# RWKV-7's triangular inverse: from GpSimd steps by way of DRAM to 32x32 products on TensorE, with other durations in the kernel's ordering estimate

## The chip, the core and the metric

The kernel runs on one core of one Trainium2 chip. The metric is the device time of one execution in microseconds. The kernel before takes 3022.41 us (median of 3 runs, 3020.9 to 3025.26). A core has five engines with queues of their own: TensorE (PE, products into PSUM), VectorE (DVE), ScalarE (ACT), GpSimd (POOL), and SyncE (SP), whose queue issues most transfers. In the profile PEld is TensorE's loading of the stationary operand.

## The reference

One inference step of two layers over 512 tokens of a prompt and 32 tokens of a sample, 1024 features, all float32. Layer 0 is half SwiGLU, RG-LRU beside retention, memory attention, half SwiGLU. Layer 1 is half SwiGLU, RWKV-7 time mixing, memory attention, half SwiGLU. The part that the change touches is the time mixing's recurrence over 16 heads of 64 features:

```
def step(S, inp):
    r_t, w_t, k_t, v_t, kk_t, b_t = inp
    sa = jnp.einsum('bhvk,bhk->bhv', S, -kk_t)
    S = S * w_t[:, :, None, :] + sa[..., None] * b_t[:, :, None, :] + v_t[..., None] * k_t[:, :, None, :]
    return S, jnp.einsum('bhvk,bhk->bhv', S, r_t)
```

The kernel computes it by chunks of 32 tokens. Within a chunk, the corrections U of all tokens solve (I + N) U = right-hand side for each head, where N is a strictly triangular 32x32 matrix of products between tokens. So each head and chunk needs the inverse of I + N once.

## The kernel before

**Halves and streams.** The 544 tokens are two halves: A (256) and B (256 of the prompt and the 32 of the sample). Features lie on partitions, tokens in columns. Every linear layer runs over granules of weights, 128 output columns each: a transfer of 512 KB into a raw buffer (`wr`), a rounding to float32r on ScalarE, a subtraction for the low part on VectorE or GpSimd (`W<-wr,W`), then 24 products. Around layer 1's mixing A is 42 granules ahead of B, so that one half's products fill the other half's waits. There are five weight slots and three raw buffers; `wkv` borrows three slots and one raw buffer for its own tiles (`K.lend(3, 1)`) until it is through.

**The order of the work.** The program is a set of generators (tasks). A planner (`Clock.op`, `Kern.plan`, `Kern.run`) estimates when each instruction could start and gives it that time as its priority, so the estimate sets each engine's order, which of VectorE and GpSimd takes an `ett` operation, and which weights are loaded when. Its durations are formulas in `mm`, `_v`, `gtt`, `act` and others. Engines then serve their queues in that order.

**The RWKV stage.** `wkv` starts five tasks over nine blocks: four of A's with 64 tokens, four of B's with 64 tokens, and the sample's 32 tokens. A block is two chunks (the last one).

- `wkv_prep` makes decays, keys and values of a block on VectorE and ScalarE and, for each chunk, 16 products `KL x X` whose masked result lands in the lower half of `X`. Rows 96 to 127 hold N. It sends N of each chunk to DRAM (`dn`).
- `wkv_solve` loads N from DRAM so that a partition holds one head, one chunk and a quarter of the rows (`P<-dn`), sets Z to the identity, and does 31 steps of elimination, each a GpSimd product and a GpSimd subtraction. Z goes back through DRAM (`dz`) into the diagonal blocks of 128x128 tiles (`w.tb`, two of them, zeroed once), by four transfers, half of them on ScalarE's queue. It waits until the chain of two blocks before is through.
- `wkv_load` transposes keys and values for the chain.
- `wkv_chain` runs the chunks in order: right-hand side (`pr`, 16 products), ScalarE's copy to `RS`, the inverse's use (`pu`, four 128x128 products), four reads, the new state (`b1`, 16 products and four VectorE operations), the output (16 products).
- `wkv_norm` does the heads' norm and gate, mostly on GpSimd.

B's blocks come in the same tasks behind A's, and need B's projections (`event "proj"`). When A's last block is through, A goes on with its output projection, attention and feed-forward while B's blocks run.

Of the kernel before, what the change touches and what calls it, by code (L numbers as in the profile page):

```python
# [10 lines left out]
F32 = mybir.dt.float32  # L11
# [40 lines left out]
def const_arrays():  # L52
# [32 lines left out]
    c["wmask"] = m  # L85
    sg = np.ones((128, 1), np.float32)
# [16 lines left out]
class Res:  # L103
    """Things that are taken and given back, with the times from which they are free."""
# [27 lines left out]
class Line:  # L132
    """The spans of time in which an engine is taken; a later comer may fill a gap."""
# [28 lines left out]
class Clock:  # L162
    """An estimate of when instructions run, in ns: what an engine does and what its operands wait for.
    It orders the emission and the engines' queues, and nothing else rests on it."""
# [24 lines left out]
    def ready(self, outs, ins=()):  # L189
        """When the operands of a transfer are free and written."""  # L190
        t = self.now
        for ap in ins:
            c, q, f = self.area(ap)
            t = max(t, c[0, q, f].max())
        for ap in outs:
            c, q, f = self.area(ap)
            t = max(t, c[:, q, f].max())
        return t

    def renew(self, old, new):  # L200
        """A tile takes over the room of an older one."""
# [47 lines left out]
class Arena:  # L249
# [26 lines left out]
    def top(self, n):  # L276
        """The last n elements."""
# [50 lines left out]
class Arenas:  # L328
    """Several arenas as one."""
# [44 lines left out]
class Kern(Clock):  # L374
# [35 lines left out]
    def gtt(self, out, a, b, op=ALU.mult):  # L410
        self.plan("g", 150 + free_size(out) * 2.0, [out], [a, b])
        self.nc.gpsimd.tensor_tensor(out, a, b, op=op)  # L412

    def ett(self, out, a, b, op=ALU.mult, lag=0.0):
        """On the engine that is through first; GpSimd has to be ahead by some ns."""
# [5 lines left out]
        dv, dg = 70 + n / 0.96, 150 + n * 2.0  # L421
# [27 lines left out]
    def gmemset(self, out, v):  # L449
        self.plan("g", 50 + free_size(out) * 0.83, [out], [])  # L450
        self.nc.gpsimd.memset(out, v)

    def scan(self, out, a, b, ini):
        self._v(out, [a, b])
# [44 lines left out]
    def sigmoid(self, out, a, bias=None, half=None):  # L499
        """1 / (1 + exp(-a - bias)) = (1 + tanh((a + bias) / 2)) / 2; half: bias / 2."""  # L500
# [66 lines left out]
    def lend(self, slots, raws):  # L567
        """Slots and buffers of the weights for another use."""
# [9 lines left out]
    def stream(self, granules, after=(), limit=None, first=0):  # L578
        """Granules that are loaded one after another, from when the streams before them are through."""
# [5 lines left out]
    def pump(self):  # L585
        """Loads of weights and their splits, as far ahead as the room allows; when the next one can go."""
# [16 lines left out]
    def _load(self, s):  # L603
        """Loads a granule, or says when it could."""
# [46 lines left out]
    def linear(self, hf, xh, xl, kc=8, m=128):  # L651
        """One granule of the main stream against a half's split columns: a PSUM bank."""
# [49 lines left out]
def load_params(K):  # L702
    """Vectors of features as columns of one tile, by way of rows of 128 and transposes."""
# [182 lines left out]
def split(K, hi, lo, src, k=0):  # L886
    """src = hi + lo, each with the 12 bits that a float32r product takes."""
# [7 lines left out]
def load_x(K, h):  # L895
    """Rows of x by way of the room for the products, as columns and their split."""
# [52 lines left out]
def store_states(K):  # L949
    """The states that were collected as columns."""  # L950
# [102 lines left out]
def rsqrt2(K, out, v, tmp, eps=None):  # L1053
    """out = -2 / sqrt(v + eps): exp(-ln / 2) and a Newton step."""
# [135 lines left out]
def give_kv(K, *tags):  # L1190
    """Slots' space for the split keys of a head and for its split values."""
# [132 lines left out]
def setup_mix0(K):  # L1324
# [26 lines left out]
    # -8 softplus(-lam) = -8 (max(-lam, 0) + 2 atanh(u / (2 + u))), u = exp(-|lam|)  # L1351
# [148 lines left out]
def rsqrt_small(K, out, v, tmp, eps):  # L1500
    """1 / sqrt(v + eps) for few columns: a guess from the bits and three Newton steps."""
# [81 lines left out]
def setup_mix1(K):  # L1583
# [5 lines left out]
    K.wz = lc[:, 2560:2816]  # L1589
# [6 lines left out]
    K.dma(K.wmask, c["wmask"])  # L1596
    K.dma(K.sgn, c["sgn"])
# [4 lines left out]
def lora_weights(K, h):  # L1602
    """The first factors of the low-rank gates, as they are and with the mix of tokens folded in."""
# [484 lines left out]
```

## Time and profile before

| | |
|---|---|
| median of 3 runs | 3022.41 us |
| profiled execution: span of the core | 3028.7 us |
| mean granted TensorE clock over the span | 0.945 |
| PE, DVE, ACT, POOL busy | 2833.4, 1743.4, 1276.8, 830.1 us |
| products (matmul records) | 22456 |
| read from HBM, written | 313.09 MB, 13.92 MB |

The profile is one execution. An instruction stands under the line of the helper that recorded it: L395 is `mm`, L400 a transpose, L408 and L412 the two-operand operations of VectorE and GpSimd, L486 ScalarE's `act`, L491 a transfer. Tiles have their slots' names: `XHA`, `W`, `Q`, `P` and others serve several uses in turn. In the RWKV stage `LC` is Z, `P` is N and the step's product, `mm` and `ax` are PSUM banks. A group's row gives count, busy time in us, mean ns of one, the engine's idle time just before, and what ended it. A float32 product appears as two records, a float32r product as one. The granted clock is TensorE's, 1.0 being full.

### The profile page before, as it was taken

To read this page: it belongs to the slowest core of one execution; us is meant where nothing else is said; L and a number is where in the kernel's file an instruction comes from. 1 tells how busy PE (TensorE), PEld (TensorE's weight loads), DVE (VectorE), ACT (ScalarE), POOL (GpSimd) and SP (SyncE) were. 2 spreads that over 40 slices of the span, in tenths; PEclk is the share of its full clock that TensorE was granted. 3 is DMA by queue.
4 is the path that set the end of the run, shared out by engine and by line. 5 is a ranking of instruction groups with operands and counts; after the bars stand their busy time and mean duration, and the time that the engine had idled before them with its cause. 6 is when DMAs were issued, how large, how long until landed. Compare 5 with 4: busy or idle time off the path is not lost.

```text
span 3028.7 us, 54637 instructions
## 1 busy us (share of the span) xinstructions
PE 2833.4 (94%) x22456; PEld 2716.3 (90%) x22456; DVE 1743.4 (58%) x3099; ACT 1276.8 (42%) x2184; POOL 830.1 (27%) x1088
## 2 busy tenths in 40 slices
PE   9999998998999999999999898888878889999998
PEld 8999998998998999989999897776767779998997
DVE  5333337677767333365355756674675666767655
ACT  4223233665545222234244343343435455655544
POOL 2001104333313000032011212466375543422301
PEclk9999999999999999999999998788778879999999
DMA  6443443322332232322356453122223135645563
GB/s 182 126 119 115 130 119 97 88 68 81 98 98 84 85 90 84 89 87 77 90 155 179 120 168 106 39 65 62 69 73 87 49 98 174 177 141 157 169 176 93
DMA packets 626331, 330.56 MB, mean 109 GB/s; under 512 B 45480, under 2 KB 620160, under 8 KB 626080
## 3 DMA queue, kind: packets, MB, share of 16 engines
q1 hardware_dynamic: 617952, 317.06, 36.8%
q0 software_dynamic: 3488, 9.44, 1.0%
q8 instruction: 176, 2.88, 0.4%
q10 hardware_dynamic: 4640, 0.56, 0.1%
q14 instruction: 75, 0.61, 0.1%
HBM read 313.09 MB, written 13.92 MB: 108 GB/s over the span
## 4 chain that ended last, share of the span: by engine, by line
PE 66%; DVE 10%; POOL 9%; DMA 7%; ACT 5%; issue 3%; SPq 0%; ACTq 0%; DVEq 0%; POOLq 0%
PE mm L395 60%; PE ax L395 4%; POOL LC L412 3%; POOL P L412 3%; DMA P<-dn 3%; DVE W L408 2%; ACT arena L486 1%; ACT W L486 1%; DVE arena L408 1%; DMA wr<-in_ffn_up 1%; PE ax L400 1%; DVE arena L432 1%; POOL arena L412 1%; ACT L2049 1%; DVE XB L408 1%
## 5 line engine op out<-in xcount | busy, mean ns | idle before, releaser
L486 ACT ACTIVATE W<-wr 128x1024 fp32r<-128x1024 f32 (+1 forms) x558 | 577.0, 1038 | 737.4 <-PE mm L395 560.0
L408 DVE TENSOR_TENSOR W<-wr,W 128x1024 fp32r<-128x1024 f32 (+1 forms) x455 | 561.5, 1236 | 551.7 <-ACT W L486 542.8
L395 PE MATMUL mm<-XHB,W 128*128 128x288 f32 x3840 | 585.1, 302 | 14.1 <-ACT XHB L486 4.7
L395 PE MATMUL mm<-XHA,W 128*128 128x256 f32 x3840 | 538.4, 290 | 28.9 <-ACT XHA L486 11.6
L395 PEld LDWEIGHTS mm<-XHB,W 128*128 128x128 f32 x3840 | 532.4, 191 | 25.0 <-ACT XHB L486 5.8
L395 PEld LDWEIGHTS mm<-XHA,W 128*128 128x128 f32 x3840 | 499.7, 194 | 39.7 <-ACT XHA L486 16.0
L412 POOL TENSOR_TENSOR W<-wr,W 128x1024 fp32r<-128x1024 f32 (+1 forms) x103 | 251.0, 2439 | 606.2 <-ACT W L486 550.6
L395 PE MATMUL mm<-XLB,W 128*128 128x288 f32 x1984 | 318.7, 300 | 0.7 <-DVE XLB L408 0.7
L395 PE MATMUL mm<-HHB,W 128*128 128x288 f32 x1920 | 291.0, 301 | 11.4 <-ACT W L486 4.4
L395 PEld LDWEIGHTS mm<-XLB,W 128*128 128x128 f32 x1984 | 283.0, 190 | 3.2 <-DVE XLB L408 1.1
L395 PE MATMUL mm<-XLA,W 128*128 128x256 f32 x1984 | 284.7, 283 | 0.0
L395 PEld LDWEIGHTS mm<-HHB,W 128*128 128x128 f32 x1920 | 267.0, 191 | 15.0 <-ACT W L486 5.3
L395 PE MATMUL mm<-HHA,W 128*128 128x256 f32 x1920 | 265.7, 288 | 5.9 <-POOL W L412 2.2
L395 PEld LDWEIGHTS mm<-XLA,W 128*128 128x128 f32 x1984 | 259.1, 190 | 0.3 <-DVE XLA L408 0.2
L395 PEld LDWEIGHTS mm<-HHA,W 128*128 128x128 f32 x1920 | 247.1, 192 | 8.8 <-POOL W L412 2.6
L486 ACT ACTIVATE arena<-mm 128x256 f32<-128x256 f32 (+4 forms) x292 | 112.2, 387 | 305.1 <-PE mm L395 287.5
L432 DVE SCALAR_TENSOR_TENSOR arena<-mm,arena 128x288 f32<-128x288 f32 (+1 forms) x176 | 77.2, 439 | 157.7 <-PE mm L395 149.0
L395 PE MATMUL mm<-HLB,W 128*128 128x288 f32 x896 | 144.3, 301 | 0.3 <-DVE HLB L408 0.3
L412 POOL TENSOR_TENSOR P<-LC,P 128x66 f32<-128x66 f32 (+24 forms) x279 | 113.5, 407 | 84.6 <-DMA P<-dn 64.6
L395 PEld LDWEIGHTS mm<-HLB,W 128*128 128x128 f32 x896 | 130.1, 193 | 0.6 <-DVE HLB L408 0.5
L395 PE MATMUL mm<-HLA,W 128*128 128x256 f32 x896 | 129.3, 284 | 0.0
L412 POOL TENSOR_TENSOR LC<-LC,P 128x66 f32<-128x66 f32 (+24 forms) x279 | 115.0, 412 | 20.5
(426 smaller groups left out, 3612.0 us busy)
## 6 DMA issues: line engine op xcount, KB each, us to landing
wr<-in_ffn_up SPq DMA_DIRECT2D x246, 512.0 KB
wr<-in_ffn_down SPq DMA_DIRECT2D x96, 448.0 KB
wr<-in_l_w_rkv SPq DMA_DIRECT2D x48, 512.0 KB
wr<-in_ffn_down SPq DMA_DIRECT2D x40, 512.0 KB
wr<-in_l_w_in SPq DMA_DIRECT2D x24, 512.0 KB
wr<-in_l_w_out SPq DMA_DIRECT2D x24, 512.0 KB
wr<-in_xa_q SPq DMA_DIRECT2D x24, 512.0 KB
wr<-in_xa_o SPq DMA_DIRECT2D x24, 512.0 KB
```

What stands on the lines that cost most here:

```text
L395: self.nc.tensor.matmul(out, lhsT, rhs, start=start, stop=stop)
L400: self.nc.tensor.transpose(out, in_, self.ident[k0:k0 + k, k0:k0 + k])
L408: self.nc.vector.tensor_tensor(out, a, b, op=op)
L412: self.nc.gpsimd.tensor_tensor(out, a, b, op=op)
L432: self.nc.vector.scalar_tensor_tensor(out, a, s, b, op0=op0, op1=op1)
L486: return self.nc.scalar.activation(out, a, f, bias=bias, scale=scale, **kw)
L2049: nc.scalar.preload_act_table_set(name)
```

## The change

The inverse no longer leaves the chip's core memories. `wkv_solve` computes N and its transpose by products of its own (`KL`, `X`, 16 heads in four column strips) into two halves of a PSUM bank, 32x32 tiles on four diagonal positions of the array, masks them by position with a new constant `winv`, and builds the inverse by products: within tiles of 8 by three factors, then two steps that join tiles of 8 to 16 and 16 to 32. There are 11 products of all tiles in seven rounds after the first; each round's result is read from PSUM by ScalarE or VectorE before the next. The result lies as 32x32 tiles, so the chain's `pu` uses 16 tile products in place of four full ones. There are three result buffers in place of two, and the wait is for the chain three blocks before. The transfers through `dn` and `dz` are gone.

The planner's durations change for products (a `side` divides the cost of products in tile positions), for VectorE, GpSimd, ScalarE and scans; its tuned margins stay. In `wkv_prep` some products go to VectorE or GpSimd by the estimate (`ett`) in place of VectorE, and the two low-rank gates take one PSUM bank after the other. The solve shares the preparation's two banks (`w.ps = w.pb`). Comments and docstrings that go are left out.

```diff
+    r, k = np.arange(32)[:, None], np.arange(32)[None, :]
+    same = lambda n: r // n == k // n
+    inv = np.stack([-1 * ((k > r) & same(8)), -1 * ((k < r) & same(8)), (k > r) & same(16) & ~same(8), (k > r) & ~same(16), r == k],
+                   1).astype(np.float32)
+    c["winv"] = np.tile(inv, (4, 1, 1))
...
-    def mm(self, out, lhsT, rhs, start=True, stop=True):
+    def mm(self, out, lhsT, rhs, start=True, stop=True, side=1):
         n = free_size(rhs)
         if lhsT.dtype == F32R:
-            cost = (n if n >= 256 else max(4 * n, 128)) / 2.4 + 2
+            cost = n / 2.4 + 13 if n >= 256 else max(4 * n / 2.4, 108.0) + 2
         else:
-            cost = 4 * (max(n, 62) / 2.4) + 2
+            cost = max(4 * n / 2.4, 108.0) / side + 2
...
-        self.plan("v", 70 + free_size(out) / (1.92 if fast else 0.96), [out], ins)
+        self.plan("v", 147 + free_size(out) / (1.92 if fast else 0.96), [out], ins)
...
-        self.plan("g", 150 + free_size(out) * 2.0, [out], [a, b])
+        self.plan("g", 190 + free_size(out) * 2.1, [out], [a, b])
...
-        dv, dg = 70 + n / 0.96, 150 + n * 2.0
+        dv, dg = 147 + n / 0.96, 190 + n * 2.1
...
-        self.plan("g", 50 + free_size(out) * 0.83, [out], [])
+        self.plan("g", 95 + free_size(out) * 0.86, [out], [])
...
-        self._v(out, [a, b])
+        self.plan("v", 195 + free_size(out) * 2.0, [out], [a, b])
         self.nc.vector.tensor_tensor_scan(out, a, b, ini, op0=ALU.mult, op1=ALU.add)
...
-        dur = (60 if a.space == PSUM else 100) + free_size(out) / 1.2
-        dur += 93 * ((bias is not None and not isinstance(bias, float)) + (not isinstance(scale, float)))
+        dur = (165 if a.space == PSUM else 204) + free_size(out) / 1.2
+        dur += 88 * ((bias is not None and not isinstance(bias, float)) + (not isinstance(scale, float)))
...
-    K.wz = lc[:, 2560:2816]
+    K.winv = lc[:, 2560:2720].rearrange("p (k t) -> p k t", k=5)
...
+    K.dma(K.winv, c["winv"])
...
-    nb = yield from K.ar2.take((1024,))
-    w.nb = nb.aps[0]
+    nb = yield from K.ar2.take((1280,))
+    w.nb, w.tb[2] = nb.aps[0][:, :1024], nb.aps[0][:, 1024:]
...
+    w.ps = w.pb
...
-        two = yield from w.pb.take(2)
-        for j in range(8):
-            for ps, q in zip(two, (0, 64)):
+        for q, t, nm in ((0, a1, "w0"), (64, a3, "a0")):
+            ps = yield from w.pb.take()
+            for j in range(8):
                 K.mm(ps[:, j * L:j * L + L], K.w2a2[q:q + 64, j * 128:j * 128 + 128], h.tw[q:q + 64, t0:t0 + L])
...
-            yield K.ready([], [X[96:128]])
-            K.dma(w.dn[b % 2][c].rearrange("h s t -> s h t"), X[96:128, :, 32:64])
...
     for b, (h, t0, L) in enumerate(w.blk):
         nch = L // 32
+        n = 128 * nch
         yield event(K, "kb", b)
-        yield lambda: b < 2 or event(K, "chain", b - 2).set
...
+        yield lambda: b < 3 or event(K, "chain", b - 3).set
...
+        def product(out, left, right):
+            for g in range(4 * nch):
+                for q in range(4):
+                    u = slice(32 * q, 32 * q + 32)
+                    K.mm(out[u, g], left[u, g], right[u, g], side=4)
...
+        ps, up, lo = yield from bank()
+        for c in range(nch):
+            X, KL = w.ck[b, c][:2]
+            for hd in range(16):
+                g, q = divmod(hd, 4)
+                u = slice(32 * q, 32 * q + 32)
+                K.mm(up[u, 4 * c + g], KL[0:64, hd, 32:64], X[0:64, hd, 32:64], side=4)
...
+        K.tt(dt, up, m(0))
+        K.tt(d, lo, m(1))
+        K.tt(et, up, m(2))
+        K.tt(ft, up, m(3))
+        w.ps.give(ps)
+        K.gtt(idt, dt, m(4), ALU.add)
+        yield
+        ps, p, pt = yield from bank()
+        product(p, dt, d)
+        product(pt, d, dt)
...
+        K.act(d2, both)
+        K.tt(id2, p, m(4), ALU.add)
+        w.ps.give(ps)
+        yield
+        ps, p, pt = yield from bank()
+        product(p, d2[:, 1], d2[:, 0])
+        product(pt, id2, idt)
+        K.tt(id4, p, m(4), ALU.add)
+        K.act(gt, pt)
...
+        product(p, gt, id4)
+        product(pt, id4, gt)
...
+        K.act(t8, both)
...
+        product(p, et, t8[:, 0])
+        K.tt(iw, m(4), p, ALU.subtract)
...
+        product(p, t8[:, 1], iw)
+        product(pt, iw, t8[:, 1])
...
+        K.act(t16, both)
...
+        product(p, ft, t16[:, 0])
+        K.tt(iw2, m(4), p, ALU.subtract)
...
+        product(p, iw2, t16[:, 1])
+        K.act(cut(w.tb[b % 3]), p)
+        w.ps.give(ps)
         event(K, "prep", b).fire(K)
...
         for g in range(4):
-            K.mm(pu[:, g * 64:g * 64 + 64], TB[:, 4 * c + g], RS[:, g])
+            for q in range(4):
+                u = slice(32 * q, 32 * q + 32)
+                K.mm(pu[u, g * 64:g * 64 + 64], TB[u, 4 * c + g], RS[u, g], side=4)
```

More of the change, by code (lines that the diff above doesn't have):

```diff
@@ L1745, in wkv @@
         units(K, w, t, 1152)
-    tb = K.slot(tags[2], [128, 2, 8, 128])
-    w.tb = [tb[:, 0], tb[:, 1]]
-    w.z = K.wz.rearrange("p (i t) -> p i t", i=8)
+    tb = K.slot(tags[2], [128, 2048])
+    w.z = [tb[:, k:k + 256] for k in range(0, 1536, 256)]
     nt = K.slot("P1", [128, 1152])
-    w.n, w.t = nt[:, 0:1024].rearrange("p (s t) -> p s t", s=32), nt[:, 1024:]
-    K.gmemset(tb, 0.0)
+    w.z2 = [nt[:, 0:512], nt[:, 512:1024]]
+    w.tb = [tb[:, 1536:1792], tb[:, 1792:2048], None]
     w.y = [K.slot("Q0", [128, 16, 64]), raws[0].rearrange("p a (b v) -> p (a b) v", v=64)]
-    w.dn = [K.drp.tile([2, 16, 32, 32], F32, name="dn%d" % k) for k in range(2)]
-    w.dz = [K.drp.tile([2, 16, 32, 32], F32, name="dz%d" % k) for k in range(2)]
     w.blk = [(A, 64 * b, 64) for b in range(4)] + [(B, 64 * b, 64) for b in range(4)] + [(B, 256, 32)]
@@ L1878, in wkv_solve @@
         nch = L // 32
-        m = nch * 16
+        n = 128 * nch
         yield event(K, "kb", b)
-        yield lambda: b < 2 or event(K, "chain", b - 2).set
-        Z, N = w.z, w.n
-        dn = w.dn[b % 2].rearrange("c h s t -> (c h) s t")
-        yield K.ready([N], [dn])
-        if nch == 2:
-            K.dma(N, dn[None].to_broadcast([4, m, 32, 32]))
-        else:
-            for g in range(4):
-                K.dma(N[g * 32:g * 32 + m], dn[:m])
-        K.gmemset(Z, 0.0)
-        for g in range(4):
-            K.gmemset(K.wz[g * 32:g * 32 + 32, g::36], 1.0)
@@ L1907, in wkv_solve @@
-        dq = w.dz[b % 2].rearrange("c (g q) s t -> q s (c g) t", q=4)
-        yield K.ready([w.tb[b % 2]], [dq])
-        for q in range(4):
-            (K.dma, K.adma)[q % 2](w.tb[b % 2][32 * q:32 * q + 32, :4 * nch, 32 * q:32 * q + 32], dq[q, :, :4 * nch])
-        yield K.done()
+        yield lambda: b < 3 or event(K, "chain", b - 3).set
+        view = lambda t: t.rearrange("p (g t) -> p g t", t=32)
+        cut = lambda t: view(t[:, :n])
+        m = lambda k: K.winv[:, k:k + 1].to_broadcast([128, 4 * nch, 32])
@@ new lines, in bank @@
+        def bank():
+            ps = yield from w.ps.take()
+            return ps, cut(ps[:, :256]), cut(ps[:, 256:])
+        ps, up, lo = yield from bank()
[5 more added lines that the diff above has]
+                K.mm(up[u, 4 * c + g], KL[0:64, hd, 32:64], X[0:64, hd, 32:64], side=4)
+            for hd in range(16):
+                g, q = divmod(hd, 4)
+                u = slice(32 * q, 32 * q + 32)
+                K.mm(lo[u, 4 * c + g], X[0:64, hd, 32:64], KL[0:64, hd, 32:64], side=4)
@@ new lines, in wkv_solve @@
+        product(p, d2[:, 1], d2[:, 0])
[3 more added lines that the diff above has]
+        w.ps.give(ps)
+        yield
+        ps, p, pt = yield from bank()
+        product(p, gt, id4)
+        product(pt, id4, gt)
+        both = ps.rearrange("p (s n) -> p s n", s=2)[:, :, :n].rearrange("p s (g t) -> p s g t", t=32)
+        K.act(t8, both)
+        w.ps.give(ps)
+        yield
+        ps, p, pt = yield from bank()
+        product(p, et, t8[:, 0])
@@ new lines, in wkv_solve @@
+        K.tt(iw, m(4), p, ALU.subtract)
+        w.ps.give(ps)
+        yield
+        ps, p, pt = yield from bank()
+        product(p, t8[:, 1], iw)
+        product(pt, iw, t8[:, 1])
+        both = ps.rearrange("p (s n) -> p s n", s=2)[:, :, :n].rearrange("p s (g t) -> p s g t", t=32)
+        K.act(t16, both)
+        w.ps.give(ps)
+        yield
+        ps, p, pt = yield from bank()
+        product(p, ft, t16[:, 0])
+        K.tt(iw2, m(4), p, ALU.subtract)
+        w.ps.give(ps)
+        yield
@@ L1912, in wkv_solve @@
+        ps, p, pt = yield from bank()
+        product(p, iw2, t16[:, 1])
+        K.act(cut(w.tb[b % 3]), p)
+        w.ps.give(ps)
         event(K, "prep", b).fire(K)
+        yield
 def wkv_load(K, w):
@@ L1980, in wkv_chain @@
             g, q = divmod(hd, 4)
-            K.mm(pr[32 * q:32 * q + 32, g * 64:g * 64 + 64], X[0:96, hd, 32:64], Y[0:96, hd])
+            K.mm(pr[32 * q:32 * q + 32, g * 64:g * 64 + 64], X[0:96, hd, 32:64], Y[0:96, hd], side=4)
         K.act(RS, pr.rearrange("p (g v) -> p g v", g=4))
```

41 lines of the change are left out of this document (16 added, 25 removed).

## The prediction

> **What bounds the kernel now.** I read the page first, for the engines and the clock, then a table of three stretches, then the chain of waits inside the middle stretch.
>
> ```profile
> span 3028.7 us, 54637 instructions
> PE 2833.4 (94%) x22456; PEld 2716.3 (90%) x22456; DVE 1743.4 (58%) x3099; ACT 1276.8 (42%) x2184; POOL 830.1 (27%) x1088
> PEclk9999999999999999999999998788778879999999
> ```
> ```profile
> core 0: us, PE busy (x) PEld busy (x) DVE busy (x) ACT busy (x) POOL busy (x), PEclk, DMA share, GB/s
> 0.00:1890.00 1890.00, 1812.34 (x14020) 1784.30 (x14021) 1006.12 (x1865) 739.66 (x1276) 360.74 (x332) 0.98 0.38 110
> 500.00:1000.00 500.00, 462.94 (x3480) 447.97 (x3479) 352.82 (x904) 269.82 (x543) 161.72 (x160) 0.96 0.29 86
> 1890.00:2490.00 600.00, 507.87 (x4422) 429.15 (x4421) 391.87 (x724) 257.50 (x477) 334.28 (x670) 0.80 0.26 66
> 2490.00:3028.70 538.70, 513.17 (x4019) 502.80 (x4017) 345.40 (x511) 279.58 (x431) 135.03 (x86) 0.98 0.53 155
> ```
>
> TensorE is the bound of the whole program. What is not bound by it lies in 1890 to 2490, the RWKV stage: the recurrence of half A, then that of half B, with the other half's linear products poured in between. I measure every stage by one quantity: PE's busy time times its granted clock, which is its work at full clock. The stage does 507.9 x 0.80 = 406 us of work in 600 us, so 194 us (32%) is lost, about half by idling and half by the low clock. The stretch 500 to 1000, mixer 0 with its own recurrences, loses 500 - 462.9 x 0.96 = 56 us, 11%. Before 1890 the loss is about 114 us, after 2490 about 36.
>
> The clock belongs to the idling, as two stretches of the stage show:
>
> ```profile
> 2132.00:2163.00 31.00, 28.11 (x315) 24.74 (x314) 25.28 (x37) 17.18 (x32) 12.29 (x7) 0.99 0.31 90
> 2240.00:2278.00 38.00, 22.19 (x212) 17.41 (x212) 32.24 (x66) 14.33 (x29) 29.85 (x64) 0.50 0.10 28
> ```
>
> Where PE is busy 91% of the time it has its full clock; where it is busy 58%, half of it. A stage that is filled better is paid twice.
>
> Now who holds the stage up: the chain of waits inside it, what GpSimd waited for, and the inverse itself (its issues that read the first DRAM copy, and its two kinds of steps).
>
> ```profile
> by line: PE mm L395 18.6%; POOL LC L412 14.6%; POOL P L412 14.5%; DMA P<-dn 14.2%; issue 6.1%; PE ax L395 5.6%; POOL HLA L412 3.0%; DVE W L408 2.7%; DMA dn<-W 2.5%; DMA dz<-LC 2.4%; PE ax L400 2.3%; POOL W L412 1.7%; ACT arena L486 0.9%; PO
> ```
> ```profile
> POOL P L412 <- DMA P<-dn: 64.6, 9, 10.7
> POOL LC L451 <- DMA dz<-LC: 38.1, 8, 5.0
> ```
> ```profile
> L491 SPq DMA_DIRECT2D P<-dn x12: 345/540/627, 1900.7 to 2439.8; - x12
> L412 POOL TENSOR_TENSOR LC<-LC,P 128x66 f32<-128x66 f32 (+24 forms) x279 | 115.0, 412 | 20.5
> L412 POOL TENSOR_TENSOR P<-LC,P 128x66 f32<-128x66 f32 (+24 forms) x279 | 113.5, 407 | 84.6 <-DMA P<-dn 64.6
> L412 POOL TENSOR_TENSOR W<-wr,W 128x1024 fp32r<-128x1024 f32 x19 | 46.2, 2434 | 41.8 <-ACT W L486 31.9 <-issue 8.4 <-DMA W<-dz 1.4
> ```
>
> The inverse (POOL LC, POOL P and the dn and dz trips) is 14.6 + 14.5 + 14.2 + 2.5 + 2.4 = 48% of the chain. Nine blocks begin theirs between 1900.7 and 2439.8: 67 us apart on average. GpSimd serves in order, so while it waits for a trip (102.7 us in all), the weight splits queued behind (W<-wr,W) wait too.
>
> **The change part by part.**
>
> *Removed.* 558 GpSimd steps, 228.5 us; the dn and dz transfers with their issues on SP's and ScalarE's queues; 103 us of GpSimd's waits. None of this is PE's time; it counts only through the loss.
>
> *Added on PE.* Per block of 64 tokens: 32 products for each of the two copies of N, then 11 products of 32 tiles: 64 + 352 = 416; the last block has half. 8 x 416 + 208 = 3536 float32 products of 32 x 32. No row has this form. The nearest is the chain's own 96-row, 32-column product, also four to a bank in four column strips (a chunk's 16 products are 32 records, so two records each):
>
> ```profile
> 1982.23 0.43 PE L395 MATMUL ax<-wr,XLA 96*32 96x64 f32 x16
> 2146.03 0.65 PE L395 MATMUL ax<-wr,W 96*32 96x64 f32 x32
> 2218.80 2.08 PE L395 MATMUL mm<-XLB 64*64 64x64 f32 x32
> 1996.65 0.80 PE L395 MATMUL ax<-wr,XLA 64*64 64x64 f32 x20
> 1906.35 3.61 PE L395 MATMUL mm<-SUMA,LC 64*128 64x64 f32 x32
> ```
>
> Sixteen more records cost 0.22 us, 14 ns each, and a burst costs 0.21 us besides. So a product is 28 ns and the work 3536 x 0.028 = 99 us, plus 8 rounds x 9 blocks x 0.21 = 15: **+114 us**. The lower bound is half of 28, 50 us, should the halved moving side (32 columns against 64) halve a record. The upper bound is products that take the same place one after another: 2.08 / 32 = 65 ns a record, 130 a product, 460 us. Between them two at a time, 0.80 / 20 = 40 ns a record, 80 a product. I take 28: same strip width, same bank use. The last row above warns: there the products alternate between upper and lower rows of the array, and a record still takes 3.61 / 32 = 113 ns. Different rows alone brought no overlap. Those fill all 128 columns, though; the new tiles differ in columns too.
>
> *Also on PE.* The inverse's use: 68 full products become 272 tile products.
>
> ```profile
> L395 PE MATMUL ax<-arena,W 128*128 128x64 f32 x128 | 19.5, 305 | 0.8 <-DMA W<-dz 0.8
> ```
>
> Two records each: 19.5 x 0.80 / 64 = 0.24 us of work, 17 us for 68, against 272 x 0.028 + 17 x 0.21 = 11: **-5 us**, between -10 and +15 by the bounds above.
>
> *Added on the other engines.* A block has eight reads of a 128x256 half bank on VectorE and five copies on ScalarE, three of them of a whole bank:
>
> ```profile
> L486 ACT ACTIVATE arena<-ax 128x256 f32<-128x256 f32 x18 | 6.7, 372 | 5.0 <-PE ax L395 2.8 <-DVE arena L408 2.2
> L486 ACT ACTIVATE arena<-ax 128x512 f32<-128x512 f32 x8 | 4.7, 587 | 4.3 <-PE ax L395 4.3
> L408 DVE TENSOR_TENSOR XA<-XA,mm 128x256 f32<-128x256 f32 x8 | 3.2, 413 | 1.4 <-PE mm L395 1.4
> ```
>
> That is 3.3 and 2.5 us a block, 30 and 22 us in all, on engines busy 392 and 258 of the stage's 600 us: covered, as long as they are not what PE waits for. The preparation may move half of its chunk products from VectorE to GpSimd, which is now free; about even. The mask's transfer, the renamed slot and the third buffer of the inverse cost nothing: the mask is loaded a layer ahead, and the buffers take room that held N and Z.
>
> *The new pace.* A block's inverse alone: 13 us of PE (416 x 0.028 + 8 x 0.21), about 5 us of reads on the path, and I allow 2 for hand-overs: 20 us. But the eight rounds alternate with filler. A granule of 24 records (rows below, 0.149 each) is a burst of 3 us; a round meets half of one, 1.5, and half a 1 us split on ScalarE, so 2 us a round: some 36, and 40 with preparation sharing the two banks. Against it stands 66 us between B's blocks (four intervals; 1900.7 to 2439.8 includes A's wait for B's projections).
>
> ```profile
> 1982.85 2.24 PE L395 MATMUL mm<-XHB,W 128*128 128x288 f32 x15
> ```
>
> A's part of the stage hardly shortens: B's blocks start only when B's projections are through, and these pass through two weight slots (three of five are lent to the stage, as before); I take 15 us. B's four intervals give 4 x 26 = 104. The stage becomes about 600 - 15 - 104 = 481 us and denser. Its loss share should fall from 32% towards the 11% of 500 to 1000; I take 14%, 67 us: **-127 us**. Its bounds: 24% of 540 us (130, -64) and 9% of 440 us (40, -154). What filler does not fit is done afterwards at full clock, and costs what it cost.
>
> *The ordering estimate.* It decides every queue's order in the whole program. Its costs rise by 77 ns an instruction on VectorE and 105 on ScalarE, to near the rows above (a 256-column read was 273 ns, now 378; the row says 372). Outside the stage 150 us are lost, partly to instructions queued for a moment that came later. I take a tenth: **-15 us**, between -50 and +30, since the waiting margins tuned on the old costs stay.
>
> Sum: +114 - 5 - 127 - 15 = -33, on the profiled 3028.7 us. That execution lies 6 us above the median of the runs shown, 3022.4, so I forecast 3022 - 33 = 2989, rounded up by 3 for the warning row: **2992**.
>
> **The rivals.**
>
> *Tiles are cheaper and the order better.* 14 ns a product (-50 us) with loss as forecast: 2940. For it: 64-column products with 32 moving columns share their places already. Against: no row shows a record under 14 ns. The Trainium skill's page "TensorEngine Tiling (Array Packing)", section Instruction Overhead, says that a product of one column takes as long as one of 60; by that rule halving the moving side saves nothing, and this rival has only the ordering left. No run here shows 32 columns on 32.
>
> *The tiles run two at a time or less* (slower). The diagonal tiles lie in different rows of the array and write one bank. At 80 ns a product the work is 283 + 15 us, 184 more than forecast: 3175; were all of the 67 us still lost to cover it, 3110. It decides from 37 ns a product on, where 33 us are used up (33 / 3536 = 9 ns more). For it: the row at 113 ns. The Trainium skill's same page, Gotcha 1: PSUM Pressure, states that different row tiles cannot access one PSUM bank at once. Taken literally, that is this rival at its worst, one after another.
>
> *The rounds stall PE* (slower). PE serves in order: at each of 72 rounds the next products wait for a read on ScalarE or VectorE, behind a 1 us split, and all filler queued behind waits too. If the loss stays at 24% of 540 us, 130, the saving is 64 instead of 127: 3055. It decides from 21% of 481 us on, where 33 us more are lost. For it, PE's longest waits in the stage today, each with the count and the longest behind it:
>
> ```profile
> PE ax L395 <- ACT HLB L486: 14.2, 4, 9.9
> PE mm L395 <- POOL W L412: 13.2, 4, 7.3
> PE mm L395 <- DVE W L408: 12.4, 9, 2.7
> ```
>
> They are waits for ScalarE's results and for splits, 1 to 4 us each. Against: two of the three kinds are waits for weight splits, which a free GpSimd shortens.
>
> *The inverse was not what paced the filler.* Two slots and B's projections set the stage; it stays at 555 us and loses 17%, 94 us: -100 + 114 - 20 = -6, with the rounding 3019, no change.
>
> **How the numbers follow.** Forecast 0.46 (own range 2970 to 3015), cheaper tiles 0.14, slow tiles 0.09, stalls 0.18, no effect 0.13. The range goes from below the cheap tiles with some ordering gain, 2925, to above the stalls, 3075. This kernel can't tell 0.2% (6 us) from no change. Faster: 0.40 of the forecast's 0.46, 0.14, and 0.04 of the last: 0.58. Slower: 0.09 + 0.18, 0.02 of the forecast's and 0.03 of the last: 0.32. Same: the other 0.10.
>
> **What would show it.** Right: no dn and dz, GpSimd between 100 and 170 us in the stage; some 7000 new 32*32 records at 14 ns in bursts; blocks of B about 40 us apart; the stage's clock near 0.9 and the loss near 67 us; PE's busy time higher, the span shorter. Wrong: bursts of 64 records longer than 1.1 us; PE idle after ScalarE in front of 32*32 products; blocks still 60 us apart, now behind the preparation; or a change outside 1890 to 2490 that outweighs the stage.

## The result and the profile after

The changed kernel takes 3144.59 us (median of 4 runs, 3140.74 to 3146.86), the kernel before 3023.2 us beside it (4 runs). The ratio is 1.0402, with a 95% interval from 1.0387 to 1.0416: 121 us slower, where 30 us faster was forecast. All of it arises in the RWKV stage.

The first two answers are of the changed kernel: lines of its page, and the table of stretches that the prediction used for the kernel before. (Helper lines stand 6 further down: `mm` is L401, ScalarE's `act` L492, VectorE L414, GpSimd L418.)

```profile
span 3142.2 us, 68992 instructions
PE 2922.5 (93%) x29936; PEld 2792.5 (89%) x29936; DVE 1782.7 (57%) x3112; ACT 1306.9 (42%) x2230; POOL 658.3 (21%) x552
PEclk9999999999999999999999997987888888999999
HBM read 307.60 MB, written 11.69 MB: 102 GB/s over the span
```
```profile
core 0: us, PE busy (x) PEld busy (x) DVE busy (x) ACT busy (x) POOL busy (x), PEclk, DMA share, GB/s
0.00:1890.00 1890.00, 1810.61 (x13981) 1780.58 (x13981) 999.81 (x1847) 735.58 (x1267) 367.36 (x331) 0.98 0.37 109
500.00:1000.00 500.00, 462.70 (x3491) 448.07 (x3491) 355.03 (x899) 270.48 (x544) 170.01 (x161) 0.96 0.29 86
1890.00:2490.00 600.00, 493.46 (x9839) 424.12 (x9837) 381.04 (x657) 245.17 (x446) 148.65 (x121) 0.84 0.18 51
2490.00:3142.20 652.20, 618.47 (x6134) 587.80 (x6120) 401.87 (x609) 326.17 (x517) 142.31 (x101) 0.93 0.46 135
```

The transfers are gone (written from 13.92 to 11.69 MB), and so are the GpSimd steps (148.65 us in place of 334.28 in 1890 to 2490). PE has 7480 records more. Before 1890 and in 500 to 1000 next to nothing has changed. But the stage now ends far behind 2490, so fixed bounds don't compare it. From here on, **the stage** is the time from the first product of A's first block to the last output product of the chain; it is read from the timeline of each kernel. Its two parts, A's blocks and B's, and the whole, first before, then after:

```profile
1886.50:2160.50 274.00, 238.61 (x2067) 198.80 (x2067) 179.92 (x326) 115.41 (x208) 149.19 (x295) 0.83 0.24 60
2160.50:2512.70 352.20, 294.81 (x2631) 254.32 (x2631) 228.70 (x425) 157.14 (x293) 193.21 (x381) 0.79 0.28 76
1886.50:2512.70 626.20, 533.42 (x4698) 453.12 (x4698) 408.62 (x750) 272.55 (x500) 342.40 (x675) 0.81 0.27 69
```
```profile
1881.90:2278.00 396.10, 320.03 (x5923) 275.60 (x5922) 250.10 (x421) 161.72 (x290) 97.57 (x80) 0.81 0.19 54
2278.00:2628.00 350.00, 313.87 (x6398) 266.42 (x6399) 207.81 (x370) 151.31 (x276) 78.31 (x65) 0.85 0.21 59
1881.90:2628.00 746.10, 633.90 (x12319) 542.02 (x12320) 457.92 (x790) 313.03 (x566) 175.88 (x145) 0.83 0.20 56
```

Measured as in the prediction (busy time times granted clock is work, the rest is lost), the stage goes from 626 us = 432 of work + 194 lost to 746 us = 526 + 220. So 94 us of the 120 are more work of PE inside the stage, and 26 are more loss, where 127 less had been promised. (The clock has two digits, so these sums are good to 3 or 4 us.) The 94 are not all new work: the longer stage also takes in 142 more records of the linear layers (the groups `mm<-..,W 128*128` count 1447 before and 1589 after), about 20 us of filler that the kernel before does outside of the stage. Summed over the whole program, with the clock recorded at each moment, PE's work grows by some 80 us (2694 to 2775) and the loss by 33 (335 to 368).

All the growth stands in A's part, 274 to 396 us; B's part is as long as it was. A's part ends with B's first product. A's last use of the inverse begins at 2180.6 in place of 2151.5, and B's first product follows it after 98 us in place of 9: in between PE does A's output projection (`mm<-HHA,W`), and B's last projections, which B's blocks wait for, come behind it.

The chain of waits inside the changed kernel's stage, and PE's longest waits there:

```profile
by line: PE mm L401 32.7%; PE ax L401 10.7%; DVE W L414 3.9%; ACT arena L492 3.3%; DVE arena L438 3.0%; PE ax L406 2.9%; issue 2.3%; ACT W L492 2.1%; DVE arena L414 2.0%; DVE XHB L414 1.9%; DMA wr<-in_l_w_out 1.7%; POOL HLA L418 1.4%; DVE X
```
```profile
PE mm L401 <- ACT W L492: 19.5, 8, 5.8
PE ax L406 <- DVE HLA L414: 14.1, 3, 9.7
PE ax L401 <- ACT arena L492: 8.2, 4, 3.3
```

The 48% that GpSimd and its transfers held of this chain are gone, as meant. PE's own products have taken their place, and the longest single wait among these, 9.7 us, is no longer than the 9.9 of the kernel before. So the question is why removing what held half of the chain gave nothing back.

### The profile page after: what moved, and what is told of

Same layout as the page of the kernel before. It is cut to its first block, busy times and chain, and to the rows that moved or that the text cites. A ratio compares the mean times of both kernels' runs of the same rounds, so it can differ in the third digit from the quotient of the medians.

```text
span 3142.2 us, 68992 instructions
## 1 busy us (share of the span) xinstructions
PE 2922.5 (93%) x29936; PEld 2792.5 (89%) x29936; DVE 1782.7 (57%) x3112; ACT 1306.9 (42%) x2230; POOL 658.3 (21%) x552
## 3 DMA queue, kind: packets, MB, share of 16 engines
HBM read 307.60 MB, written 11.69 MB: 102 GB/s over the span
## 5 line engine op out<-in xcount | busy, mean ns | idle before, releaser
L414 DVE TENSOR_TENSOR W<-wr,W 128x1024 fp32r<-128x1024 f32 (+1 forms) x456 | 566.7, 1244 | 603.0 <-ACT W L492 600.5
L492 ACT ACTIVATE W<-wr 128x1024 fp32r<-128x1024 f32 (+1 forms) x558 | 578.0, 1039 | 733.5 <-PE mm L401 568.5
L401 PE MATMUL mm<-XHB,W 128*128 128x288 f32 x3840 | 579.8, 300 | 12.7 <-DVE XHB L449 4.5
L401 PE MATMUL mm<-XHA,W 128*128 128x256 f32 x3840 | 547.2, 293 | 28.0 <-ACT XHA L492 11.1
L401 PEld LDWEIGHTS mm<-XHB,W 128*128 128x128 f32 x3840 | 530.0, 190 | 21.3 <-DVE XHB L449 4.7
L401 PEld LDWEIGHTS mm<-XHA,W 128*128 128x128 f32 x3840 | 505.7, 196 | 42.4 <-ACT XHA L492 15.7
L418 POOL TENSOR_TENSOR W<-wr,W 128x1024 fp32r<-128x1024 f32 (+1 forms) x102 | 243.0, 2383 | 1013.0 <-ACT W L492 912.1
L401 PE MATMUL mm<-XLB,W 128*128 128x288 f32 x1984 | 313.5, 298 | 0.0
L401 PE MATMUL mm<-HHB,W 128*128 128x288 f32 x1920 | 294.4, 303 | 7.3 <-POOL W L418 3.2
L401 PE MATMUL mm<-XLA,W 128*128 128x256 f32 x1984 | 294.7, 287 | 4.0 <-DVE XLA L414 3.8
L401 PEld LDWEIGHTS mm<-XLB,W 128*128 128x128 f32 x1984 | 280.2, 189 | 1.6 <-issue 1.0
L401 PEld LDWEIGHTS mm<-HHB,W 128*128 128x128 f32 x1920 | 268.4, 192 | 13.5 <-POOL W L418 4.2
L401 PE MATMUL mm<-HHA,W 128*128 128x256 f32 x1920 | 271.5, 290 | 2.8 <-ACT W L492 1.8
L401 PEld LDWEIGHTS mm<-XLA,W 128*128 128x128 f32 x1984 | 262.6, 191 | 6.9 <-DVE XLA L414 4.2
L401 PEld LDWEIGHTS mm<-HHA,W 128*128 128x128 f32 x1920 | 250.7, 194 | 7.1 <-ACT W L492 2.0
L492 ACT ACTIVATE arena<-mm 128x256 f32<-128x256 f32 (+4 forms) x295 | 113.6, 387 | 322.3 <-PE mm L401 311.4
L401 PE MATMUL mm<-HLB,W 128*128 128x288 f32 x896 | 143.5, 300 | 0.0
L401 PEld LDWEIGHTS mm<-HLB,W 128*128 128x128 f32 x896 | 128.9, 192 | 0.7 <-issue 0.5
L401 PE MATMUL mm<-HLA,W 128*128 128x256 f32 x896 | 129.5, 284 | 0.0
L414 DVE TENSOR_TENSOR arena<-arena 128x256 f32<-128x256 f32 (+3 forms) x130 | 92.6, 715 | 46.6 <-ACT arena L492 42.6
L418 POOL TENSOR_TENSOR arena<-arena 128x256 f32<-128x256 f32 (+3 forms) x82 | 81.9, 1001 | 171.6 <-DVE arena L438 86.9
```

The lines of the kernel that those rows point to most:

```text
L401: self.nc.tensor.matmul(out, lhsT, rhs, start=start, stop=stop)
L414: self.nc.vector.tensor_tensor(out, a, b, op=op)
L492: return self.nc.scalar.activation(out, a, f, bias=bias, scale=scale, **kw)
```

## The experiments

Times are of single runs where nothing else is said; the kernel before took 3017 to 3026 us beside them. The stage's row is shown where the verdict rests on it.

### What an inverse costs at all

Both kernels were run without any inverse: a constant's copy, or the zeroed tiles, stand where the result would be read.

```diff
-        for s in range(31):
-            nr, nt = s // 4 + 1, 31 - s
-            T = w.t[:, :nr * nt].rearrange("p (i t) -> p i t", i=nr)
-            K.gtt(T, Z[:, :nr, s:s + 1].to_broadcast([128, nr, nt]),
...
```

> The kernel before without its inverse: the DRAM trips and the 31 GpSimd steps a block are left out and the chain multiplies by zero tiles (so the recurrence's numbers are wrong). Theory 2 (the inverse was cover, not cost): the stage is held by its preparation and by two weight slots, so PE's lost time stays near 190 us between A's first block and B's last output, and the time is 2990 to 3020 us. Rival (the chain of waits is the price): the inverse's 48% of that chain goes, the stage shrinks by 100 us or more, and the time is below 2930 us.

Measured: **2972.73 us**, between the two expectations. In the changed kernel, the eight rounds gave way to one copy:

```diff
-        ps, up, lo = yield from bank()
...
-        K.act(cut(w.tb[b % 3]), p)
-        w.ps.give(ps)
+        K.act(cut(w.tb[b % 3]), m(4))
```

> The changed kernel without the inverse: one ScalarE copy of the identity mask stands for it (the tile products and their reads are left out, so the recurrence's numbers are wrong). Theory 1 (order): even with the inverse at no cost, A's stage ends before B's projections and its output projection comes in between; it takes 3030 to 3080 us, above the kernel before. Rival (rounds): without the rounds nothing is slow, and the time is 2900 to 2960.

Measured: **3039.42 us**, as the first of the two expected. The stage of e5, then of e4:

```profile
1880.20:2445.40 565.20, 507.20 (x4650) 432.20 (x4652) 408.18 (x745) 273.10 (x496) 111.39 (x78) 0.83 0.20 60
```
```profile
1887.30:2530.20 642.90, 552.36 (x5383) 478.88 (x5381) 444.27 (x716) 301.73 (x535) 187.27 (x144) 0.82 0.23 67
```

The GpSimd inverse, 48% of the stage's chain, costs the old kernel 3019 - 2973 = 47 us in all (3019 is the kernel before beside that run). Without it the stage still loses 565 - 507.2 x 0.83 = 144 us of its 194; the chain falls to its next links. The tile inverse costs the new kernel 3145 - 3039 = 105 us: by these rows 526 - 453 = 73 us of work and 30 of loss in the stage, and over the whole program, where filler that moved in or out of the stage cancels, 85 of work and 20 of loss. An inverse that adds that much work on PE could win only by doing most of it in time that PE loses anyway; e9 below shows that added products are not absorbed so. And the two kernels without an inverse differ by 67 us.

### The ordering estimate, and what any new order costs

The change's durations alone, in the kernel before; then the reverse, the changed kernel with the old ones:

```diff
-        self.plan("v", 70 + free_size(out) / (1.92 if fast else 0.96), [out], ins)
+        self.plan("v", 147 + free_size(out) / (1.92 if fast else 0.96), [out], ins)
...
```

> The kernel before (inverse on GpSimd, two DRAM trips, its preparation unchanged) with only the new durations in the ordering estimate. Theory 1 (order): the loss of 120 us lies between A's first block and B's first block, because B's last projection granules come to stand behind A's output projection in the two weight slots; the estimate of this kernel has B's projections ready at the same time as A's stage, so it should take 3000 to 3040 us, with B's first block products near 2160 us. Rival (estimate): the new durations by themselves order the program worse; then 3100 us or more.

> The changed kernel with the old durations of VectorE, ScalarE, GpSimd and float32r products in the estimate; the division of a tile product's cost by four stays. Theory 1 (order): the estimate still puts B's projections some 85 us behind A's stage, so 3110 to 3160 us and B's first block products near 2270 us. Rival (estimate): the loss goes with the durations, 2990 to 3040 us.

Measured: 3052.38 us (34 slower than before, between its two expectations) and 3122.64 us (22 faster than after). Read alone, this says that the durations cost 20 to 35 us. The next runs change them without meaning, by 1, 2 or 4 ns an instruction:

```diff
-        self.plan("v", 70 + free_size(out) / (1.92 if fast else 0.96), [out], ins)
+        self.plan("v", 72 + free_size(out) / (1.92 if fast else 0.96), [out], ins)
...
-        dur = (60 if a.space == PSUM else 100) + free_size(out) / 1.2
+        dur = (62 if a.space == PSUM else 102) + free_size(out) / 1.2
```

> The kernel before, with 2 ns more in the ordering estimate's cost of every VectorE and ScalarE instruction: a change without meaning, which can only exchange instructions whose moments almost tie. If the 34 us that the new durations cost by themselves come from what they say, this stays within 10 us of 3,020 us. If any other order costs as much, it is 3,030 us or more.

> The kernel before, with 4 ns more in the ordering estimate's cost of every VectorE and ScalarE instruction. If the 32 us of the 2 ns run are what any disturbance of this kernel's order costs: 3,040 to 3,065 us. If that run was a single bad draw: within 10 us of 3,020.

> The same with 1 ns more. As for 4 ns: 3,040 to 3,065 us if any disturbance loses an order that was a lucky or a chosen one; within 10 us of 3,020 if the smallest disturbance leaves it.

Measured: 2 ns **3053.92**, 4 ns **3057.09**, 1 ns **3046.9** us. Four disturbances of the old kernel's order, the true durations among them, all land between 3047 and 3057. So the durations themselves cost nothing that can be told; what is lost is the order that the kernel before happens to have, 29 to 40 us better than its four neighbours. The stage with 2 ns, and PE's longest waits in it:

```profile
1883.60:2532.80 649.20, 526.62 (x4722) 450.78 (x4722) 417.82 (x755) 274.60 (x503) 334.82 (x675) 0.80 0.26 68
```
```profile
PE ax L400 <- DVE HLA L408: 26.0, 3, 12.9
PE mm L395 <- POOL W L412: 14.3, 4, 6.2
PE ax L395 <- DMA W<-dz: 11.2, 2, 6.8
```

The same instructions lose 649 - 421 = 228 us in place of 194; PE's idle time in the stage goes from 93 to 123 us. The first row has grown most: three waits, 26 us together, for a result of VectorE (`HLA`) that comes late in this order. In the kernel before the same kind was

```profile
PE ax L400 <- DVE HLA L408: 4.3, 2, 2.4
```

A few such waits are enough. Then the same disturbance on the other kernels:

> The changed kernel, with 2 ns more in the ordering estimate's cost of every VectorE and ScalarE instruction. If 3,145 us is an ordinary draw of the new kernel: 3,130 to 3,160 us. If the 22 to 37 us that undoing the durations, the shared bank or the preparation's engine gave were only another order: 3,105 to 3,125 us, as they gave.

> The same with 4 ns more, and the same two cases: 3,130 to 3,160 us if 3,145 is an ordinary draw, 3,105 to 3,125 us if it was an unlucky one.

> The kernel before without its inverse (as in the run before it of that kind, the inverse is left out and the identity's copy stands in its place), with 2 ns more in the ordering estimate's VectorE and ScalarE costs. If 2,973 us is an ordinary draw without an inverse: 2,965 to 2,985 us. If removing the inverse kept a lucky order: 3,000 to 3,015 us, and then a free inverse would have been worth only 10 to 20 us against the kernel before, and 40 to 50 against its placebos.

Measured: **3143.24**, **3139.51** and **3007** us. The changed kernel's time is an ordinary draw. The old kernel without inverse (with zeroed tiles, as in e5) also moves by 34 us; with both disturbed, the GpSimd inverse costs 3054 - 3007 = 47 us, as it did in the old order (47).

So the result falls into four steps of measured runs: 3022 to 2973 (the GpSimd inverse goes, -49), 2973 to 3007 (the old order goes, +34), 3007 to 3039 (the rest of the change: durations, preparation, tile products in `pu`; +32), 3039 to 3145 (the tile inverse, +105). The runs without an inverse are single draws, so each step carries the scatter that the disturbed orders show, up to 40 us for these kernels; the third is not clear of it.

### The tile products themselves

```diff
                     K.mm(out[u, g], left[u, g], right[u, g], side=4)
+                    K.mm(out[u, g], left[u, g], right[u, g], side=4)
```

> The changed kernel, but each tile product of the inverse's eleven doubling and joining products is issued a second time, with the same operands, so the output is the same. That is 2,992 products (5,984 records) more, and no read, copy or wait more. Theory that PE's work is the price and a product takes about 16 ns at full clock and twice that at half: +50 to +100 us, so about 3,220 us. Rival, that the price lies in the waits between the rounds and the products are nearly free: within 20 us of 3,145. If the second products did not run side by side (80 ns each): +240 us or more.

Measured: **3313.26 us**, +169, far outside of what was expected. The stage of this run, and PE's longest waits in it:

```profile
1880.30:2803.10 922.80, 782.16 (x18437) 676.88 (x18437) 460.75 (x806) 328.11 (x579) 176.75 (x143) 0.78 0.17 50
```
```profile
PE mm L401 <- issue: 64.4, 42, 2.4
PE mm L401 <- ACT W L492: 12.0, 7, 4.5
```

Work in the stage is 782.2 x 0.78 = 610 us, 84 more for 2992 products, so at most 28 ns each (some filler fits into the longer stage); over the whole program the work grows by 64 us, 21 ns each. The loss is 313 us against 220, and this the expectation had not seen. PE stands 64 us in front of products for which the profile names no releaser, where the changed kernel has next to none of this. But other waits shrank: its idle time rises only from 112 to 141 us, and the larger part of the added loss is the lower clock, 0.78 in place of 0.83. The changed kernel's rows of the tile products, and bursts in its timeline:

```profile
L401 PE MATMUL mm<-W 32*32 32x32 f32 x2720 | 38.0, 211 | 15.2 <-ACT W L492 14.1 <-DVE W L414 0.7 <-issue 0.3
L401 PE MATMUL mm<-P,W 32*32 32x32 f32 x2176 | 27.7, 200 | 0.7 <-DVE W L414 0.5
L401 PE MATMUL ax<-arena,W 32*32 32x64 f32 x384 | 9.1, 240 | 5.7 <-ACT arena L492 5.7
L401 PE MATMUL ax<-arena,arena 32*32 32x64 f32 x160 | 3.2, 217 | 0.0
```
```profile
2316.06 2.00 PE L401 MATMUL mm<-SUMB,LC 64*128 64x64 f32 x16
...
2374.20 0.63 PE L401 MATMUL ax<-arena,W 32*32 32x64 f32 x32
2374.65 1.23 PE L401 MATMUL mm<-W 32*32 32x32 f32 x120
...
2381.22 3.67 PE L401 MATMUL mm<-SUMB,LC 64*128 64x64 f32 x16
...
2391.71 1.08 PE L401 MATMUL mm<-P 32*32 32x32 f32 x64
...
2394.88 1.02 PE L401 MATMUL ax<-HLB,centt 128*128 128x512 f32 x2
2401.69 1.93 PE L401 MATMUL mm<-W 32*32 32x32 f32 x128 [5.78 <-ACT W L492]
...
2408.28 0.75 PE L401 MATMUL mm<-P,W 32*32 32x32 f32 x64
...
2413.07 0.71 PE L401 MATMUL mm<-P,W 32*32 32x32 f32 x62
...
2417.96 0.75 PE L401 MATMUL mm<-P,W 32*32 32x32 f32 x64
...
2421.50 0.75 PE L401 MATMUL mm<-P,W 32*32 32x32 f32 x64
2422.19 1.14 PE L401 MATMUL mm<-W 64*64 64x64 f32 x16
```

Sixty-four records, 32 products, take 0.75 us with the burst's end, and 120 take 1.23, both at a granted clock of 1.00. So 56 more records take 0.48 us, 8.6 ns each: a product is 17 ns, although all write one bank; products of 64 columns that take the same place one after another were 130 ns in the prediction's rows. They were cheaper than forecast. (The burst of 128 in 1.93 us ran at a clock of 0.50.) The timeline also shows one block's seven product rounds, 2374.1 to 2422.2: **48 us**, in which PE spends some 9 on them; the eight full blocks took 35 to 55 us, 46 in the mean. From the first round to the second it is 17 us, from there to the third 10: in the first gap PE does products of the chain and of the preparation that the order puts there, in the second it stands 5.78 us for ScalarE's copy. The first gap holds one thing more: PE is busy without a break in it, and has half its clock:

```profile
2381.00:2391.00 10.00, 10.00 (x62) 8.45 (x64) 5.30 (x9) 4.26 (x8) 0.73 (x1) 0.50 0.00 0
```

Sixteen records of `mm<-SUMB,LC` take 3.67 us there, and 2.00 at 2316, where the clock is 1.00. So at half clock the same work keeps PE busy about twice as long, and a high busy share can hide a low clock.

The next block's products (`mm<-W 64*64`) come right behind the last round; inverse and preparation draw from the same two banks.

### Banks, order of the projections, slots, preparation

A bank each for preparation and inverse:

```diff
-    w.ps = w.pb
+    w.pb, w.ps = Res(K, m2[:1]), Res(K, m2[1:])
```

> The changed kernel with one PSUM bank for the preparation and one for the inverse, in place of two that both draw from. Theory 3 (banks): the preparation's products of a block run at the inverse's end because the inverse holds both banks; with a bank of its own the preparation moves ahead, blocks come 55 us apart in place of 71, and the time is 3090 to 3120 us. Theory 2 (TensorE's added work is the price): 3130 to 3155 us.

> The changed kernel with a PSUM bank each for preparation and inverse, with 2 ns more in the same costs. If the 36 us come from the banks: 3,100 to 3,120 us. If they were another order: 3,130 to 3,150 us.

Measured: **3108.8** and, with 2 ns more, **3128.49** us, the second between its two expectations: 16 to 36 faster than after, so about half of the first figure may be its order. The stage of e8, then with 2 ns more:

```profile
1879.00:2586.60 707.60, 648.90 (x12204) 543.17 (x12206) 457.07 (x785) 303.75 (x553) 168.69 (x136) 0.84 0.19 54
1888.00:2603.00 715.00, 649.99 (x12179) 544.44 (x12179) 447.97 (x774) 304.25 (x553) 184.71 (x146) 0.83 0.19 53
```

PE's idle time falls in both, from 112 us to 59 and 65. But the clock hardly gains: PE is busy in 648.9 of 707.6 us, 92%, and yet has a clock of 0.84.

A's output projection held back until B's projections are through:

```diff
     yield event(K, "wkv", h.name)
+    if not isb:
+        yield event(K, "proj", "B")
     unlimit(h.solo)
```

> The changed kernel, but A's stream of weights goes on to its output projection only when B's projections are through (one more wait on an event of the ordering program). Theory 1 (order): B's first block products move from 2278 us back to about 2180, and the time from 3145 to 3030 to 3060 us. Rival (rounds): the stage is slow because its eight rounds and the shared banks stall it; then B's projections are late anyway and the time stays above 3110.

Measured: 3149.58 us. In the timeline B's first block then starts at 2222 in place of 2278, and the end doesn't move. So the late start of B's blocks behind A's output projection, where most of the growth of A's part stands, was not what the time hung on: what is not done there is done later.

The third weight slot given back to the filler, without an inverse, and with the GpSimd inverse in compact 32x32 tiles:

```diff
-    slots, raws = yield from K.lend(3, 1)
+    slots, raws = yield from K.lend(2, 1)
```

> As e4 (the changed kernel, a ScalarE copy of the identity in place of the inverse, numbers wrong), but the stage borrows two weight slots in place of three, so the filler has three. Theory 2a (slots): the filler is what starves PE; PE's lost time in the stage falls from 182 us in e4 to about 120, and the time from 3039 to 2960 to 2990 us. Theory 2b (preparation and chain): the time stays within 15 us of 3039.

> The kernel before with its GpSimd inverse, kept as 32x32 tiles of 256 columns in place of zeroed 128x128 blocks (the chain uses 16 tile products, as in the changed kernel), so that a third weight slot stays with the filler. Theory 2a (slots): 2960 to 2995 us. Theory 2b (preparation and chain): 3005 to 3030 us.

Measured: 3014.7 us (25 under e4) and 3058.47 us (39 over before), both outside of what was expected. After the disturbed runs both are inconclusive: 25 us is within what such kernels scatter by, and 3058 is about what the old kernel takes in the four disturbed orders.

The preparation on VectorE alone:

```diff
-                f = K.tt if e else K.ett
+                f = K.tt
...
```

> The changed kernel, but the preparation of a block does its elementwise products on VectorE alone, as the kernel before does, and none on GpSimd. Theory that VectorE and GpSimd slow each other there (VectorE's 256-column product takes 416 ns alone and 1.2 to 2.7 us beside GpSimd's): 3,110 to 3,130 us. Rival, that this part of the change is about even, as the prediction said: within 10 us of 3,145.

Measured: 3107.53 us, 37 faster. Some of VectorE's products in the stage, after, and then in this run:

```profile
L414 DVE TENSOR_TENSOR W<-HLB,arena 64x256 f32<-64x256 f32 x8 | 9.4, 1196 | 0.1
L414 DVE TENSOR_TENSOR XHB<-HLB,arena 64x256 f32<-64x256 f32 x3 | 8.0, 2662 | 0.1
L414 DVE TENSOR_TENSOR W<-arena 64x256 f32<-64x256 f32 x12 | 4.8, 416 | 0.1
```
```profile
L414 DVE TENSOR_TENSOR W<-HLB,arena 64x256 f32<-64x256 f32 x10 | 5.7, 566 | 0.1
L414 DVE TENSOR_TENSOR XHB<-HLB,arena 64x256 f32<-64x256 f32 x4 | 2.7, 684 | 0.0
```

Products of the same shape take 0.42 us in the quickest group, and up to 2.66 on average of three in the changed kernel. With GpSimd out of the preparation most of that is gone. Together with the old durations and a bank each:

> The tile products with three parts of the change taken back: the ordering estimate has its old durations, preparation and inverse have a PSUM bank each, and preparation is on VectorE. One by one the first two gave -22 and -36 us. Theory that the tile products cost PE more work than the GpSimd inverse ever cost in lost time (47 us): 3,065 to 3,095 us, still slower than the kernel before. Rival, that the tile inverse is sound and only its surroundings cost: below 3,020 us.

Measured: 3110.75 us (4 runs), ratio to before 1.0292, 95% interval from 1.0275 to 1.031; slower than both expectations. Three edits that gave 22, 36 and 37 us alone give 34 together, and e8 and e10 reach the same 3108. Each of the three is below all draws of the changed kernel (3140 to 3150), but which of them removes what can't be told from these runs. With every correction that was found the tile inverse stands at 3108 to 3128 us, 55 to 75 above the old kernel in a disturbed order. No version that computes the inverse was faster than the kernel before.

## Why the prediction was wrong

**The step that failed: "Its loss share should fall from 32% towards the 11% of 500 to 1000; I take 14%, 67 us: -127 us."** The stage loses 220 us, not 67. Three things stood under it, and none held.

- *The inverse as the pace.* The prediction read 48% of the chain of waits as what paces the stage. Without any inverse the loss falls by 50 us (194 to 144) and the time by 47. That was about the most that any inverse could give, and less than half of the +109 that the forecast itself charged. The chain tells who ended last, not how far behind the next one is; the loss of 500 to 1000, whose recurrences have other filler, was no floor for this stage.
- *The pace of 40 us a block.* The rounds of a block took 46 us on average in place of 36 (a granule's burst, put at 3 us there, is 24 x 0.149 = 3.6), and those of B's five blocks began between 2313 and 2584, four intervals of 68 us, as before (66). The 104 us that these intervals were to give gave nothing: B's part stayed at 350 us. A's part was to shorten by 15 us and grew by 122: the first products of A's blocks came 75 us apart in place of 52, and B's projections came later. The wait behind preparation in the shared banks, named there with 4 us a block, is worth 16 to 36 us in all by e8 and e18.
- *"A stage that is filled better is paid twice."* In e8 PE is busy 92% of the stage and the clock is 0.84; the row behind that sentence had 91% and 0.99. Nor is that the tile products' doing alone: e5, which has none, shows 90% and 0.83. Of the two halves of the loss it is mainly one that moves: the idle half is 93 us before and 58 and 59 in e5 and e8, and the half lost to the low clock (busy time times what is missing to 1.0) is 101, 86 and 104. The stretch from 2381 to 2391 shows why the busy share was a poor guide.

**The products: right in kind, too dear.** 28 ns forecast, 17 measured in a long burst; products and `pu` together cost some 80 us of work over the whole program, against +114 - 5. The rival of slow tiles fell: 64 records took 0.75 us, where two at a time would take 2.6. The Trainium skill's page "TensorEngine Tiling (Array Packing)", Gotcha 1, read as that rival read it, one product after another, does not hold in that row, where products of four row tiles went into one bank at 17 ns each. What the prediction took from the Instruction Overhead of the Trainium skill's same page, that halving the moving side saves nothing, did not hold either: on the same four positions 32 records with 64 columns take 0.63 us, and 64 records with 32 columns 0.75. Whether the Trainium skill's figure itself, a latency, is wrong these rows don't say. **The inverse's use** was about right: 9.1 + 3.2 us busy in place of 20.5 before, at the stages' clocks 6 us of work less, where 5 were forecast.

**The ordering estimate: -15 forecast.** With the right durations the old kernel takes 34 us more, but so it does with meaningless ones (29 to 40). The step asked what better durations win; what counted was that each of the four new orders lost some 33 us. The bounds, -50 to +30, nearly held it.

**Covered work: partly wrong.** "About even" for preparation on GpSimd: undone, it gave 37 us in one run, with VectorE's products back from 1.2 to 0.57 us. The Trainium skill's page "SBUF — State Buffer", section "SBUF: two separate sides", says that VectorE's operations with two operands there and GpSimd's operations that read there lock each other out for a whole instruction; the rows of e10 agree. How much of the 37 us is this, and how much another order, is open.

**The rivals.** The nearest was "the inverse was not what paced the filler", with 13%: it let the stage shrink by 45 us only (600 to 555), and e5, without any inverse, shrinks it by 61 (626 to 565). Its own sum still came to 3019, since it took 100 us off the loss while the work was added; even e5 took off only 50. "The rounds stall PE" shows in its rows, 15.2 + 5.7 us in front of tile products, and is a sixth of the 121. It had the loss fall to 130 us, and the loss rose to 220.

## What to carry to other kernels

Before replacing what heads a chain of waits, run the kernel with it left out: that one run is about the ceiling of every replacement, and here it would have ended the matter at 47 us against the 109 us of new work that the forecast itself put on the engine that bounds the program. Where a planner orders the queues, first disturb its numbers without meaning and measure the scatter; the kernel at hand may sit at the lucky end of it, and then every edit is charged for leaving that place. Effects smaller than the scatter need several draws on both sides.

## What the runs showed of the hardware that had not been expected

- Float32 products of 32x32 on the four diagonal positions run side by side into one PSUM bank: 8.6 ns a record in a long burst (56 records in 0.48 us), where 32 records with 64 moving columns on these positions take 0.63 us.
- Twice as many of them in a row left PE waiting 64.4 us in 42 waits of up to 2.4 us for nothing that the profile names, with transfers of the instruction queue at 281 in place of 234 (176 in the kernel before):

```profile
q8 instruction: 281, 4.60, 0.6%
```

  That instructions were late would fit, but no run shows it.
- The granted clock of the stage hardly rose with PE's busy time, with tile products or without: 0.82 at 86% (e4), 0.83 at 90% (e5), 0.84 at 92% (e8). From 2381 to 2391 of the changed kernel PE was busy all of 10 us at a clock of 0.50. What the clock counts as busy was not settled.
